# An f32 encoder layer on one core: other PSUM banks for two kinds of tile, two gain buffers, 8-block steps in the down products, and SiLU as one instruction

## The chip, the cores and the metric

The kernel runs on one core of one Trainium2 chip. The metric is device time in microseconds (us). The engines have their own instruction queues and run side by side: PE (TensorE) multiplies matrices into PSUM, DVE (VectorE) and ACT (ScalarE) work element by element, POOL (GpSimd) does a few small ones, SP (SyncE) issues the DMAs. PSUM has eight banks here, each of them one tile of 128x512 f32.

## The reference

One layer on 256 tokens of width 2048, all in f32:

```
h += 1/2 * post(SwiGLU_1(pre(h)))          # 2048 -> 5632 -> 2048
h += post(W_o [norm(NA heads) | norm(dilated heads)])   # q/k/v: 2048 -> 3*2048
h += 1/2 * post(SwiGLU_2(pre(h)))
h += post(sigmoid(pre(h) W_g) * (p W_p))   # p: 256 tokens x 256

swiglu(u)  = (silu(u @ w_gate) * (u @ w_up)) @ w_down
pre, post  = RMSNorm with a gain per column
```

The mixer has 16 heads of width 128 in four groups of four: the first group is a neighbourhood attention with a position bias, the other three a mixture of dilated windows with rotary positions. Every head's output is normalised before `W_o`.

## The kernel before, in words

Every product of weights has the 256 tokens in two halves (t = 0, 1) as the stationary operand and 512 columns of a weight as the moving one. To keep f32 precision each operand is split into a high part (a cast to the reduced type `F32R`) and a low part (the rest), and a block of 128 rows costs three matmuls: high x high (line 90), low x high (91), high x low (92). `split` does this for two row blocks of a weight: the cast `wh` on ACT (line 72), the difference `wl` on DVE (line 73). Six such pairs of buffers exist. The weights arrive by DMA as `raw` (line 64), in tiles of up to four row blocks.

`product` runs over the row blocks in steps: it loads and splits the step's blocks, then takes all of them for t = 0 and all of them for t = 1. A step has 8 blocks (`SUPER`) unless the caller gives `steps`. `mid` is a function that is called shortly before the last blocks of t = 1, when the sum of t = 0 is complete. Work put into `later` is issued behind the next step.

A feed-forward block takes the 5632 hidden columns in eleven pieces of 512, in four groups of 3, 3, 3 and 2. All but the first piece use `pair_product`, which for the first four row blocks computes gate and up together, with seven block products instead of eight, by sums and differences of operands; it has four short sums (`x = bank("x")`, each used up at once) and four long ones (v, z, y, x). `gated` then makes `silu(x) = x * sigmoid(x)`, with the row factor `rs[t]` of the norm in `scale`. Behind each group come its down products, four blocks of 512 columns each (loop over `b`), added up in `f`. In the last group, `down_out` also takes the squares of `f` on ACT and multiplies by the post-norm's gain, which one DMA per column block brings (`gain`). `residual` is a generator that goes on from there: the factor of the norm (DVE, POOL), the update of `h` (line 328), its transposes on PE (`tr`, line 239), the gain `y_g`, and the two parts `u_h` (245) and `u_l` (246) for the next stage.

In the attention stage each group of heads does q, k and v by `product`, then `attend` for each t and each pair of heads: scores `sc` (line 504), bias and maximum on DVE (`sb`, 511), exponential on ACT (`pr`, 515), transposes `pt` (521), their copy `pts` (523), and the sum over values `o` (527), for which a tile is taken from the pool `ps_acc`.

At the start, `load_x` brings the transposed x in eight pieces of two row blocks and makes the two parts of `x * gain` while the first product runs: a product on DVE (`xg`, line 297), a cast on ACT (298), a difference on DVE (299). The pieces of the first four row blocks are kept (`x_first`) for the sums that `pair_product` needs (`token_sums`).

The order of the instructions on each engine is not written by hand: a scheduler sets it from the program, the dependencies and the free buffers. So a pool with other counts of buffers changes the order. PSUM before: six banks in `ps_acc`, used in turn by all products, the pair sums and `o`; two in `ps_tr` for scores and transposes.

## Time and profile before

| | us |
|---|---|
| median of 3 runs | 1985.33 (1981.21 to 1986.32) |
| the profiled execution | 1985.5 |
| its span, first to last instruction | 1983.5 |
| PE busy | 1947.0 |
| DVE busy | 1371.2 |
| ACT busy | 992.0 |
| first matmul at | 6.11 |

Rows of instructions have the start in us, the length in us, engine, line, operation, result <- operands, shapes and count; in brackets the idle time of the engine before it and what ended it. Rows of groups have the count, then busy time in us and mean ns of one, then the idle time before them. Busy PE is drawn by modelled ends: successive matmuls overlap in the rows. PEclk is the clock that PE was granted, 1 being full.

### The profile page before, as it was taken

To read this page: it belongs to the slowest core of one execution; us is meant where nothing else is said; L and a number is where in the kernel's file an instruction comes from. 1 tells how busy PE (TensorE), PEld (TensorE's weight loads), DVE (VectorE), ACT (ScalarE), POOL (GpSimd) and SP (SyncE) were. 2 spreads that over 40 slices of the span, in tenths; PEclk is the share of its full clock that TensorE was granted. 3 is DMA by queue.
4 is the path that set the end of the run, shared out by engine and by line. 5 is a ranking of instruction groups with operands and counts; after the bars stand their busy time and mean duration, and the time that the engine had idled before them with its cause. 6 is when DMAs were issued, how large, how long until landed. Compare 5 with 4: busy or idle time off the path is not lost.

```text
span 1983.5 us, 22804 instructions
## 1 busy us (share of the span) xinstructions
PE 1947.0 (98%) x8840; PEld 1612.7 (81%) x8840; DVE 1371.2 (69%) x1526; ACT 992.0 (50%) x1206; POOL 26.5 (1%) x47
## 2 busy tenths in 40 slices
PE   8999999999999999999999999999999999999998
PEld 6888888888888878788888878888888888888786
DVE  6874787578757776566565587747875787577764
ACT  6554554355435446544535465545543554354563
POOL 0000000000000000000000000000000000000000
PEclk9999999999999999999999999999999999999999
DMA  9666556555655546454453665555565556555453
GB/s 336 212 211 201 170 191 226 177 191 170 233 170 191 191 163 214 130 198 139 138 202 127 219 211 186 210 198 171 191 229 174 191 170 233 170 190 191 170 195 119
DMA packets 190348, 376.91 MB, mean 190 GB/s; under 512 B 6432, under 2 KB 9504, under 8 KB 189984
## 3 DMA queue, kind: packets, MB, share of 16 engines
q1 hardware_dynamic: 190240, 375.46, 55.8%
q8 instruction: 69, 1.13, 0.2%
q14 instruction: 39, 0.32, 0.0%
HBM read 373.33 MB, written 2.10 MB: 189 GB/s over the span
## 4 chain that ended last, share of the span: by engine, by line
PE 95%; DMA 2%; ACT 1%; DVE 1%; issue 0%; POOL 0%; SPq 0%; DVEq 0%; POOLq 0%; ACTq 0%
PE down L90 8%; PE down L91 8%; PE down L92 8%; PE pair_x L90 5%; PE pair_x L91 5%; PE pair_x L92 5%; PE pair_z L92 3%; PE pair_y L90 3%; PE pair_z L90 3%; PE pair_z L91 3%; PE pair_y L92 3%; PE pair_y L91 3%; PE pair_v L90 3%; PE pair_v L91 3%; PE pair_v L92 3%; PE tr L239 2%
## 5 line engine op out<-in xcount | busy, mean ns | idle before, releaser
L73 DVE TENSOR_TENSOR wl<-raw,wh 128x1024 fp32r<-128x1024 f32 (+1 forms) x753 | 908.9, 1221 | 446.0 <-ACT wh L72 421.8
L72 ACT CAST wh<-raw 128x1024 fp32r<-128x1024 f32 (+1 forms) x753 | 790.0, 1052 | 762.2 <-PE down L91 207.9
L90 PE MATMUL down<-wh,hid_h 128*128 128x512 f32 x704 | 274.7, 391 | 0.1
L91 PE MATMUL down<-wh,hid_l 128*128 128x512 f32 x704 | 274.2, 389 | 0.0
L92 PE MATMUL down<-wl,hid_h 128*128 128x512 f32 x704 | 274.2, 389 | 0.0
L90 PEld LDWEIGHTS down<-wh,hid_h 128*128 128x128 f32 x704 | 132.2, 188 | 28.1 <-ACT hid_h L245 1.0
L92 PEld LDWEIGHTS down<-wl,hid_h 128*128 128x128 f32 x704 | 132.2, 188 | 27.4
L91 PEld LDWEIGHTS down<-wh,hid_l 128*128 128x128 f32 x704 | 132.2, 188 | 27.1
L90 PE MATMUL pair_x<-wh,u_h 128*128 128x512 f32 x320 | 124.6, 389 | 0.0
L91 PE MATMUL pair_x<-wh,u_l 128*128 128x512 f32 x320 | 124.6, 389 | 0.0
L92 PE MATMUL pair_x<-wl,u_h 128*128 128x512 f32 x320 | 124.6, 389 | 0.0
L90 PE MATMUL pair_y<-wh,u_h 128*128 128x512 f32 x280 | 109.0, 389 | 0.0
L92 PE MATMUL pair_y<-wl,u_h 128*128 128x512 f32 x280 | 109.0, 389 | 0.0
L91 PE MATMUL pair_y<-wh,u_l 128*128 128x512 f32 x280 | 109.0, 389 | 0.0
L161 DVE TENSOR_TENSOR raw<-raw 128x1024 f32<-128x1024 f32 x80 | 97.8, 1223 | 1.4
L92 PE MATMUL pair_z<-wl,u_h 128*128 128x512 f32 x240 | 93.5, 390 | 0.0
L90 PE MATMUL pair_z<-wh,u_h 128*128 128x512 f32 x240 | 93.4, 389 | 0.0
L91 PE MATMUL pair_z<-wh,u_l 128*128 128x512 f32 x240 | 93.4, 389 | 0.0
L91 PE MATMUL pair_v<-wh,u_l 128*128 128x512 f32 x240 | 93.4, 389 | 0.0
L92 PE MATMUL pair_v<-wl,u_h 128*128 128x512 f32 x240 | 93.4, 389 | 0.0
L90 PE MATMUL pair_v<-wh,u_h 128*128 128x512 f32 x240 | 93.4, 389 | 0.0
L92 PEld LDWEIGHTS pair_x<-wl,u_h 128*128 128x128 f32 x320 | 60.1, 188 | 12.5
(195 smaller groups left out, 3085.3 us busy)
## 6 DMA issues: line engine op xcount, KB each, us to landing
raw<-in_ffn_w_up SPq DMA_DIRECT2D x88, 1024.0 KB, 5.1
raw<-in_ffn_w_down SPq DMA_DIRECT2D x88, 1024.0 KB, 4.9
raw<-in_ffn_w_gate SPq DMA_DIRECT2D x84, 1024.0 KB, 5.1
raw<-in_w_qkv SPq DMA_DIRECT2D x48, 1024.0 KB, 5.1
raw<-in_w_o SPq DMA_DIRECT2D x16, 1024.0 KB, 4.9
raw<-in_w_ple_gate SPq DMA_DIRECT2D x16, 1024.0 KB, 5.0
raw<-in_ffn_w_gate SPq DMA_DIRECT2D x7, 512.0 KB, 4.8
xb<-in_xT SPq DMA_DIRECT2D x8, 256.0 KB, 4.2
```

Source lines behind the costliest of these rows:

```text
L72: nc.scalar.copy(wh[:, :n], raw)
L73: nc.vector.tensor_tensor(wl[:, :n], raw, wh[:, :n].bitcast(F32), op=ALU.subtract)
L90: nc.tensor.matmul(acc, xh, wh, start=lead, stop=False)
L91: nc.tensor.matmul(acc, xl, wh, start=False, stop=False)
L92: nc.tensor.matmul(acc, xh, wl, start=False, stop=tail)
L161: nc.vector.tensor_tensor(out_, x, y, op=ALU.add)
L239: nc.tensor.transpose(tr[:, k], x[:, k * P : (k + 1) * P], ident)
```

## The change

- PSUM: `ps_acc` has 4 banks, and a new pool `ps_o` has 2, for the short sums of `pair_product` and for the attention output `o`.
- `gpool`, the gains of the post-norms, has 2 buffers, not 1.
- The down products of the second to fourth column block take the default steps (for 12 row blocks 4 and 8, for 8 row blocks 8) instead of steps of 4.
- `gated` is one ScalarE instruction (`Silu`) instead of a sigmoid on ACT and a product on DVE.
- `load_x` makes the high part on ACT straight from x with the gain as a scale, one row block at a time, and the low part by one DVE instruction each. x of the first four row blocks is multiplied by the gain in place afterwards, for the token sums.
- Some scratch tiles have another buffer name (`y0` instead of `sq`).

```diff
-    gpool = ctx.enter_context(tc.tile_pool(name="gpool", bufs=1))
+    gpool = ctx.enter_context(tc.tile_pool(name="gpool", bufs=2))
-    ps_acc = ctx.enter_context(tc.tile_pool(name="ps_acc", bufs=6, space=PSUM))
+    ps_acc = ctx.enter_context(tc.tile_pool(name="ps_acc", bufs=4, space=PSUM))
     ps_tr = ctx.enter_context(tc.tile_pool(name="ps_tr", bufs=2, space=PSUM))
+    ps_o = ctx.enter_context(tc.tile_pool(name="ps_o", bufs=2, space=PSUM))
...
         def bank(x):
+            if x == "s":
+                return ps_o.tile([P, NB], F32, name="pair_s", tag="o")
             return ps_acc.tile([P, NB], F32, name=f"pair_{x}", tag="acc")
...
-        x = bank("x")
+        x = bank("s")
         mac(x, a11, split(ra[:, :2]), first=True, last=True)
...
-        xb = work.tile([P, 2, S], F32, name="xb", tag="hg")
+        xb = work.tile([P, 2, S], F32, name="xb", tag="y0" if k < KB else "hg")
         nc.sync.dma_start(xb, xT[:, k : k + 2])
-        xg = work.tile([P, 2, S], F32, name="xg", tag="y0" if k < KB else "sq")
-        g = row_g[:, 0, k : k + 2]
-        nc.vector.tensor_tensor(xg, xb, g.unsqueeze(2).broadcast_to([P, 2, S]), op=ALU.mult)
-        nc.scalar.copy(hi, xg)
-        nc.vector.tensor_tensor(lo, xg, hi.bitcast(F32), op=ALU.subtract)
+        for i in range(2):
+            g = row_g[:, 0, k + i : k + i + 1]
+            nc.scalar.activation(hi[:, i], xb[:, i], AF.Copy, scale=g)
+            nc.vector.scalar_tensor_tensor(
+                lo[:, i], xb[:, i], g, hi[:, i].bitcast(F32), op0=ALU.mult, op1=ALU.subtract
+            )
         if k < KB:
-            x_first.append(xg)
+            x_first.append(xb)
...
         def gated(x, t):
-            s = pool.tile([P, NB], F32, name="sig", bufs=1)
-            nc.scalar.activation(s, x, AF.Sigmoid, scale=rs[t])
             y = pool.tile([P, NB], F32, name="gs", bufs=3)
-            nc.vector.scalar_tensor_tensor(y, x, rs[t], s, op0=ALU.mult, op1=ALU.mult)
+            nc.scalar.activation(y, x, AF.Silu, scale=rs[t])
             return y
...
                         product(gate, lhs, w_gate, 0, c0, steps=steps, ahead=load_x)
+                        for i, x in enumerate(x_first):
+                            g = row_g[:, 0, 2 * i : 2 * i + 2].unsqueeze(2).broadcast_to([P, 2, S])
+                            nc.vector.tensor_tensor(x, x, g, op=ALU.mult)
...
-                product(acc, hrows, w_down, f0 * NB, b * NB, steps=[KB] * ng, mid=mid)
+                product(acc, hrows, w_down, f0 * NB, b * NB, steps=[KB] * ng if b == 0 else None, mid=mid)
...
-                o = ps_acc.tile([P, KB, HD], F32, name="o", tag="acc")
+                o = ps_o.tile([P, KB, HD], F32, name="o", tag="o")
...
-                later.append(lambda on=on, t=t: transposed_split(on, *o_split, t, g))
+                later.append(lambda on=on, t=t: transposed_split(on, *o_split, t, g, tag="y0"))
```

The change moves instructions. Three places show it; line numbers of the changed program are up to 5 higher, and the number behind a PSUM tile's name tells tiles apart.

PE in the attention stage of the second head group, behind the first scores, before:

```order
L504 MATMUL sc<-kT_l,qT_h 128x256
L521 MATMUL pt<-ident,pr 128x128 x2
L504 MATMUL sc<-kT_h,qT_h 128x256
L504 MATMUL sc<-kT_h,qT_l 128x256
L504 MATMUL sc<-kT_l,qT_h 128x256
L521 MATMUL pt<-ident,pr 128x128 x2
L504 MATMUL sc<-kT_h,qT_h 128x256
L504 MATMUL sc<-kT_h,qT_l 128x256
L504 MATMUL sc<-kT_l,qT_h 128x256
L527 MATMUL o<-v,pts 128x128 x4
```

And now, from the last of the six q matmuls behind the scores on:

```order
L93 MATMUL q_6743<-wl,u_h 128x512
L526 MATMUL pt<-ident,pr 128x128 x2
L509 MATMUL sc<-kT_h,qT_h 128x256
L509 MATMUL sc<-kT_h,qT_l 128x256
L526 MATMUL pt<-ident,pr 128x128 x2
L509 MATMUL sc<-kT_l,qT_h 128x256
L509 MATMUL sc<-kT_h,qT_h 128x256
L509 MATMUL sc<-kT_h,qT_l 128x256
L509 MATMUL sc<-kT_l,qT_h 128x256
L91 MATMUL q_6743<-wh,u_h 128x512
L532 MATMUL o<-v,pts 128x128 x4
L92 MATMUL q_6743<-wh,u_l 128x512
```

The matmuls of the next group's q product, which stood behind the fourth pair of heads, now stand between: two row blocks (six matmuls, of which the last is shown) ahead of the first pt, twelve matmuls in the first head group, and one ahead of and one behind each o.

PE at the end of the first feed-forward block, before:

```order
L90 MATMUL down_5329<-wh,hid_h 128x512
L91 MATMUL down_5329<-wh,hid_l 128x512
L92 MATMUL down_5329<-wl,hid_h 128x512
L239 MATMUL tr<-ident,h 128x128 x8
L90 MATMUL q_5526<-wh,u_h 128x512
```

And now:

```order
L92 MATMUL down_5290<-wh,hid_l 128x512
L242 MATMUL tr<-ident,h 128x128 x4
L93 MATMUL down_5290<-wl,hid_h 128x512
L242 MATMUL tr<-ident,h 128x128 x4
L91 MATMUL down_5290<-wh,hid_h 128x512
L92 MATMUL down_5290<-wh,hid_l 128x512
L93 MATMUL down_5290<-wl,hid_h 128x512
L91 MATMUL q_5487<-wh,u_h 128x512
```

The two transposes of h for t = 0 now stand before the last four of the 24 down matmuls for t = 1.

ACT at the start, with what each instruction waits for, before:

```order
L298 ACT_TABLE_LOAD
L298 CAST u_h<-xg 128x512 [waits DVE_49]
L72 CAST wh<-raw 128x512 [waits DMAHW2_49]
L72 CAST wh<-raw 128x512 [waits DMAHW3_49]
L298 CAST u_h<-xg 128x512 [waits DVE_49]
```

And now; DMAHW1 is the first piece of x, DMAHW0 the row gains:

```order
L300 ACT_TABLE_LOAD [waits DMAHW1_49]
L300 ACTIVATE u_h<-xb,row_g 128x256 [waits DMAHW0_49]
L300 ACTIVATE u_h<-xb,row_g 128x256
L73 CAST wh<-raw 128x512 [waits DMAHW2_49]
L73 CAST wh<-raw 128x512 [waits DMAHW3_49]
L300 ACTIVATE u_h<-xb,row_g 128x256 [waits DMAHW4_49]
```

The table load waits for x now. On DVE, the token sums stand ahead of the split of row blocks 4 and 5 (the last row); before, they stood behind the last piece of x:

```order
L373 TENSOR_TENSOR xb<-xb,row_g 128x512
L258 TENSOR_TENSOR y_s<-xb 128x256
L260 TENSOR_TENSOR y_s<-xb 128x256
L259 TENSOR_TENSOR y_s<-y_s,xb 128x256
L261 TENSOR_TENSOR y_s<-xb,y_s 128x256
L264 TENSOR_TENSOR sums_l<-y_s,sums_h 128x512
L74 TENSOR_TENSOR wl<-raw,wh 128x1024
```

## The prediction

> **What bounds the kernel now.** I read the page first, then the busy time by stretches, then what TensorE (PE) waited for, then three stretches instruction by instruction.

> From the page, PE's share and the chain that ended last:

> ```profile
> PE 1947.0 (98%) x8840; PEld 1612.7 (81%) x8840; DVE 1371.2 (69%) x1526; ACT 992.0 (50%) x1206; POOL 26.5 (1%) x47
> PE 95%; DMA 2%; ACT 1%; DVE 1%; issue 0%; POOL 0%; SPq 0%; DVEq 0%; POOLq 0%; ACTq 0%
> ```

> PE sets the end. The number of its matrix instructions does not change, so time can come only from where PE pauses or runs at less than its full clock. Two starts, 21 matmuls apart, give the slot of one 128x512 matmul when nothing holds it:

> ```profile
> 1861.66 0.39 PE L92 MATMUL down<-wl,hid_h 128*128 128x512 f32 x1
> 1866.42 0.39 PE L92 MATMUL down<-wl,hid_h 128*128 128x512 f32 x1
> ```

> (1866.42 - 1861.66) / 21 = 0.227 us. Busy time by stretches (length, then PE busy; after the five engines PEclk, the granted clock) shows where slots are lost:

> ```profile
> 50.00:400.00 350.00, 350.00 (x1570) 290.44 (x1569) 251.18 (x251) 174.03 (x186) 0.00 (x0) 1.00 0.58 197
> 0.00:40.00 40.00, 32.07 (x125) 24.90 (x126) 26.85 (x36) 23.65 (x33) 1.48 (x9) 1.00 0.92 320
> 720.00:740.00 20.00, 16.36 (x69) 12.48 (x68) 15.62 (x23) 7.53 (x12) 2.81 (x4) 0.83 0.37 130
> 800.00:820.00 20.00, 16.70 (x98) 14.43 (x97) 9.57 (x26) 13.28 (x27) 1.02 (x1) 0.91 0.34 106
> 880.00:900.00 20.00, 17.83 (x111) 15.25 (x110) 9.57 (x26) 12.57 (x27) 1.01 (x1) 1.00 0.42 140
> 1860.00:1880.00 20.00, 16.62 (x72) 13.35 (x71) 13.12 (x19) 10.46 (x17) 3.29 (x4) 0.91 0.53 184
> ```

> Inside a feed-forward block PE has no gap in 350 us. The loss sits at the start, at the end of the first feed-forward block (720), in the attention stage of the first head group (800) and of the three that follow like the one at 880, and at the end of the second feed-forward block (1860). Loss = gap + (1 - PEclk) x 20: 3.6 + 3.4 = 7.0 us at 720, 3.3 + 1.8 = 5.1 at 800, 2.2 at 880, 3.4 + 1.8 = 5.2 at 1860.

> **The change part by part.**

> *Own PSUM banks for the attention output and the short pair products.* What PE waited for in attention, over all four stages (total us, times, longest), and the rows of the stage at 880:

> ```profile
> PE pt L521 <- ACT pr L515: 6.5, 4, 2.7
> PE o L527 <- ACT pts L523: 3.5, 11, 0.7
> 806.12 1.28 ACT L515 ACT_TABLE_LOAD   x1
> 886.37 1.23 DVE L73 TENSOR_TENSOR wl<-raw,wh 128x1024 fp32r<-128x1024 f32 x1
> 887.26 0.28 PE L504 MATMUL sc<-kT_l,qT_h 128*128 128x256 f32 x1
> 888.82 0.44 PE L521 MATMUL pt<-ident,pr 128*128 128x128 f32 x2 [1.28 <-ACT pr L515]
> 889.46 0.38 PE L521 MATMUL pt<-ident,pr 128*128 128x128 f32 x2
> 890.51 0.49 PE L527 MATMUL o<-v,pts 128*128 128x128 f32 x2 [0.32 <-ACT pts L523]
> 896.75 0.48 PE L90 MATMUL q<-wh,u_h 128*128 128x512 f32 x1
> 897.07 0.39 PE L91 MATMUL q<-wh,u_l 128*128 128x512 f32 x1
> ```

> After the scores (sc) PE stands until softmax (pr) is there; the longest of the four, 2.7, holds the table load of 1.28. The new order puts matmuls of the next product (q, in the last group mo) into these places: six behind the first scores (twelve in the first group), then one before and one behind each o. Six need 6 x 0.227 = 1.36 us against a wait of 1.28; twelve 2.72 against 2.7. The o waits for pts, 1.05 us after the second pt (889.46 to 890.51). In the new order two pt, four sc and one q stand between, about 0.2 + 0.5 + 0.3 = 1.0 (lengths of the starts above). So nearly all 6.5 + 3.5 = 10.0 us of waiting go. A row of 0.28 is followed after 0.11 to 0.12 when nothing holds PE, so each of the 15 waits hides about 0.16 more: 2.4. The half-rate time at 800 (1.8) should go with its wait. Against this, the first 128x512 matmul behind a narrow one takes 0.32 (896.75 to 897.07), not 0.227: 0.09 for some 6 more switches in each of 4 stages, 2.2. Sum 10.0 + 2.4 + 1.8 - 2.2 = 12.0. The weights must be split by then: the wl at 886.37 ended before the scores did, and DVE's and ACT's order in this stage is unchanged. Bounds: 6 if half of the fills come late, 12; I take **-11**.

> *Longer steps in the down products (8 row blocks, 4 for the first column block).* The token half t=0 now ends 24 matmuls before the product does, not 12. At the end of the first block:

> ```profile
> 724.03 0.69 DVE L396 TENSOR_TENSOR f<-f,down 128x512 f32<-128x512 f32 x1 [0.63 <-PE down L92]
> 725.56 0.69 DVE L399 TENSOR_TENSOR f<-f,g_post 128x512 f32<-128x512 f32 x1 [0.85 <-ACT sq L232]
> 726.32 0.39 PE L92 MATMUL down<-wl,hid_h 128*128 128x512 f32 x1
> 728.17 1.41 DVE L328 SCALAR_TENSOR_TENSOR h<-f,r,h 128x512 f32<-128x512 f32 x2 [0.44 <-POOL r L227]
> 729.02 1.71 PE L239 MATMUL tr<-ident,h 128*128 128x128 f32 x8 [2.31 <-issue]
> 731.56 0.80 PE L90 MATMUL q<-wh,u_h 128*128 128x512 f32 x1 [0.82 <-ACT u_h L245]
> 732.04 1.29 DVE L246 TENSOR_TENSOR u_l<-y_g,u_h 128x512 fp32r<-128x512 f32 x2
> ```

> From the add of f at 724.03 (call it F) to the first transpose is 4.99 us. PE began its t=1 half 0.2 before F and was out of work 2.5 after it. Now the first transpose stands behind 20 matmuls, 4.5 us: the wait falls from 2.5 to about 0.7. What is late next: from the transpose to the first q is 2.54 us, and eight transposes and four matmuls (0.9 + 0.9) cover 1.8 of it, leaving 0.7. Then u_l: in the new DVE order the add of f for t=1, which needs the product's end (F + 7.2), and an h update stand ahead of it, so u_l ends near F + 9.3 and the second q waits about 1.6. Only one split for q stands ahead of all this; the next one follows u_l and costs about 1.0. Waits of 0.7 + 0.7 + 1.6 + 1.0 = 4.0 against 7.0 lost now: 3.0 if no half-rate time follows, 1.3 if one does (the two stretches at 0.91 lost 1.8 each). I take **-2.5**, bounds 0 and -5.

> [...]

> *Two buffers for the post-norm gains.* At the end of the second block:

> ```profile
> 1859.31 0.34 SPq L217 DMA_DIRECT2D g_post<-in_ffn_post_g  x1
> 1864.12 0.69 DVE L396 TENSOR_TENSOR f<-f,down 128x512 f32<-128x512 f32 x1 [0.63 <-PE down L92]
> 1868.49 0.69 DVE L399 TENSOR_TENSOR f<-f,g_post 128x512 f32<-128x512 f32 x1 [3.68 <-DMA g_post<-in_ffn_post_g]
> 1871.99 0.63 PE L239 MATMUL tr<-ident,h 128*128 128x128 f32 x4 [3.38 <-DVE h L328]
> ```

> The gain arrived 2.8 us later in the chain than in the first block (4.37 after F instead of 1.53). With two buffers it is asked for one column block earlier, some 11 us. Then the chain is the first block's 4.99, and the wait before the transposes 0.7 instead of 3.4; behind them stand 48 matmuls of the small projection, 10.9 us, which cover u_h and u_l. Half rate (1.8) goes. 3.4 + 1.8 - 0.7 = 4.5, less some switches of 0.09: **-4**, bounds -2 and -5.

> *Start: the scaled copy on ACT.* The rows of today:

> ```profile
> 0.71 1.28 ACT L298 ACT_TABLE_LOAD   x1 [0.71 <-PEq L722]
> 3.90 0.69 DVE L297 TENSOR_TENSOR xg<-xb,row_g 128x512 f32<-128x512 f32 x1 [3.90 <-DMA xb<-in_xT]
> 5.44 1.26 ACT L72 CAST wh<-raw 128x512 fp32r<-128x512 f32 x2 [0.19 <-DMA raw<-in_ffn_w_gate]
> 6.11 0.80 PE L90 MATMUL gate<-wh,u_h 128*128 128x512 f32 x1 [6.11 <-ACT wh L72]
> 8.12 0.80 PE L91 MATMUL gate<-wh,u_l 128*128 128x512 f32 x1 [1.22 <-DVE u_l L299]
> L515 ACT ACTIVATE pr<-sb,nmax 128x256 f32<-128x256 f32 x32 | 16.0, 499 | 4.6 <-DVE nmax L511 3.4 <-DVE sso L537 1.1
> L255 DVE TENSOR_TENSOR y_s<-xg 128x256 f32<-128x256 f32 x1 | 0.4, 422 | 0.0
> L354 DVE SCALAR_TENSOR_TENSOR gs<-p,r,sig 128x512 f32<-128x512 f32 x20 | 15.0, 752 | 15.8 <-ACT sig L352 15.8
> ```

> The table load is the first ACT instruction, and in the new order it waits for the first piece of x. So: x at 3.9, load to 5.1, two scaled copies of 128x256 at 0.45 (the exponential of that size takes 0.50, and 0.62 is half of the two casts of 128x512 above) to 6.0, wh to 6.7: the first matmul comes 0.6 later. The 1.2 at 8.12 goes, because u_l no longer stands behind the next x; at half rate that frees two or three slots. But both engines' orders now have the token sums (six DVE and two ACT instructions, 4 us of DVE by 0.69 and 0.4 each) before the splits of row blocks 4 and 5, which puts PE back by 1. Together **+0.5**, bounds -1 and +2.

> *One ScalarE instruction for the gate.* It removes 44 DVE instructions (gs, the last row above) of 0.75, 33 us of DVE, and leaves 44 on ACT. PE has no wait for the gate (the 350 us without a gap hold it), so 0. If that cover were gone, the gate would be worth at most 0.75 for each of 22 blocks. ACT's order shows five table loads, not four: the sigmoid of the last stage needs its own. 1.28 on an engine busy for half of the span: 0. [...] The trace shows 1.28, and the copy that follows a load at once.

> Sum: -11 - 2.5 - 4 + 0.5 = -17, against the profiled execution's 1985.5 (span 1983.5 and 2.0 around it). The median of the runs shown is 1985.33, so the two stand together: **1968 us**.

> **The rivals.**

> *Half of the fill only* (chance 0.20). The softmax chain, not the order, sets the attention stage: a matmul put between can hold pt or o longer than the wait it fills. For it: margins of 0 to 0.1 us in the sums above. Against it: ACT and DVE are idle for a third to a half of that stretch. Attention then gives 5: 1974.

> *The ends give nothing* (0.12). The waits move from the transposes to u_h and u_l, half rate stays, and the start costs its 2. Then -11 + 2: 1976.5.

> *Longer steps starve PE* (0.04). A step of 8 holds four of the six split pairs for its whole second half; if the casts for the next step come late, each of 24 such steps (3 in each of 8 groups) waits. At 0.7 us a step the gain is gone, at 1.0 us it is +24: 1992. Against it, the same step of 8 runs today in the output projection without a gap:

> ```profile
> L90 PE MATMUL mo<-wh,hid_h 128*128 128x512 f32 x128 | 50.2, 392 | 0.0
> ```

> The casts need 4 x 1.2 us of DVE in each 10.9 us.

> *It is not one instruction* (0.02): the gate function would swap tables with the casts at each block, 88 x 1.28 us of ACT. Five loads in the order speak against it; time then over 1990.

> **How the numbers follow.** My forecast has 0.62 and its own range is 1963 to 1974. With the first two rivals the range for 8 in 10 is 1962 to 1978. A change under about 0.3% (6 us) can't be told from none here; faster than 1979.4 has 0.88 (forecast, both rivals, less their upper edges), within 0.3% 0.07, slower 0.05.

> **What would show it.** Right: in attention no wait of pt for pr over 0.3 us and the granted clock 1.00 in all four stages; before the first transposes of each block's end a wait under 1 us; no wait of DVE for a gain; the first matmul near 6.7. Wrong: waits of down matmuls for wh or wl; pt still waiting over 1 us; PE waiting over 1.5 us for u_l with the clock below 1.

## The result and the profile after

The changed kernel takes 1967.16 us (median of 4 runs, 1966.55 to 1969.06), the kernel before beside it 1984.55 (4 runs, 1981.21 to 1986.32): a ratio of 0.9916, with a 95% interval of 0.9899 to 0.9933. The profiled execution took 1969.06, its span is 1967.0, against 1985.5 and 1983.5 before. So 16.5 us of span are gone. Two executions in this document, 2800.57 us with the earlier start and 7008.73 us (the profiled one) with the old gate, were in a slow state and are left out of the times and ratios.

The page of the changed kernel, busy time by engine and the chain that ended last:

```profile
PE 1941.9 (99%) x8840; PEld 1607.5 (82%) x8840; DVE 1340.8 (68%) x1484; ACT 994.5 (51%) x1215; POOL 28.3 (1%) x47
...
PE 96%; DVE 2%; DMA 1%; ACT 0%; issue 0%; POOL 0%; SPq 0%; DVEq 0%; POOLq 0%; ACTq 0%
```

PE still sets the end. DVE has 30 us less to do. What PE waited for (total us, times, longest):

```profile
PE gate L91 <- ACT wh L73: 8.8, 2, 7.0
PE q L91 <- ACT u_h L248: 1.5, 1, 1.5
PE tr L242 <- DVE h L332: 1.0, 2, 0.5
PE q L93 <- DVE wl L74: 1.0, 1, 1.0
```

The waits of pt for pr and of o for pts, 10.0 us before, are no longer there. Busy time by stretches, at the places that the prediction spoke of (by the add of f, the end of the first block comes 1.2 us earlier now and that of the second 15.4):

```profile
0.00:40.00 40.00, 31.16 (x118) 24.57 (x119) 25.01 (x38) 24.28 (x41) 0.97 (x9) 0.96 0.90 320
720.00:740.00 20.00, 17.26 (x85) 13.25 (x84) 15.47 (x25) 7.70 (x12) 3.28 (x4) 1.00 0.46 157
800.00:820.00 20.00, 20.00 (x121) 16.92 (x120) 10.15 (x27) 13.89 (x28) 1.01 (x1) 1.00 0.32 106
880.00:900.00 20.00, 20.00 (x121) 16.98 (x121) 11.22 (x31) 12.50 (x27) 2.01 (x2) 1.00 0.32 106
...
1840.00:1870.00 30.00, 28.99 (x138) 23.69 (x137) 25.08 (x34) 19.70 (x30) 2.81 (x4) 1.00 0.55 184
```

The attention stages at 800 and 880 have no gap. The granted clock is 1.00 from 21.74 to 1960.51, behind the last matmul.

Where the time went, place by place. Loss here is a sum over the matmuls of a stretch: the time from each start to the next, less what the same width takes where nothing holds PE (0.227 us for 512 columns, 0.109 for 128, 0.119 for 256: the medians of the trace). Half rate, a granted clock of 0.50, is in it.

| loss, us | before | after | change | predicted |
|---|---|---|---|---|
| start: first matmul's time, and loss to 40 us | 11.8 | 13.3 | +1.5 | +0.5 |
| end of the first block | 7.35 | 5.50 | -1.9 | -2.5 |
| four attention stages | 16.34 | 4.55 | -11.8 | -11 |
| end of the mixer | 2.71 | 2.62 | -0.1 | not spoken of |
| end of the second block | 5.20 | 1.54 | -3.7 | -4 |

Together -16.0. The 96 score matmuls, whose median went from 0.125 to 0.119, are -0.6 more; the rest is +0.1.

The second head group's attention, after the first scores:

```profile
883.29 0.39 PE L93 MATMUL q<-wl,u_h 128*128 128x512 f32 x1
...
883.42 0.50 ACT L520 ACTIVATE pr<-sb,nmax 128x256 f32<-128x256 f32 x1
883.57 0.44 PE L526 MATMUL pt<-ident,pr 128*128 128x128 f32 x2
...
884.54 0.58 ACT L528 COPY pts<-pt 128x512 f32<-128x512 f32 x1 [0.53 <-PE pt L526]
...
884.82 0.39 PE L91 MATMUL q<-wh,u_h 128*128 128x512 f32 x1
...
885.18 1.16 PE L532 MATMUL o<-v,pts 128*128 128x128 f32 x8
```

The second head's exponential starts at 883.42, when the first's is done; pt for the first follows 0.15 later, straight behind the sixth q, and o starts 0.06 behind the end of the copy (884.54 + 0.58 = 885.12). The fill only just covers, as worked out. The end of the first block:

```profile
722.80 0.69 DVE L401 TENSOR_TENSOR f<-f,down 128x512 f32<-128x512 f32 x1 [2.34 <-PE down L93]
...
726.95 2.08 DVE L332 SCALAR_TENSOR_TENSOR h<-f,r,h 128x512 f32<-128x512 f32 x3 [0.44 <-POOL r L230]
727.80 0.63 PE L242 MATMUL tr<-ident,h 128*128 128x128 f32 x4 [0.51 <-issue]
...
728.95 1.28 DVE L246 TENSOR_TENSOR y_g<-tr,row_g 128x512 f32<-128x512 f32 x2
...
729.70 1.04 ACT L73 CAST wh<-raw 128x1024 fp32r<-128x1024 f32 x1 [1.95 <-PE down L92]
...
730.65 1.14 ACT L248 CAST u_h<-y_g 128x512 fp32r<-128x512 f32 x2
...
731.32 0.50 PE L91 MATMUL q<-wh,u_h 128*128 128x512 f32 x1 [1.48 <-ACT u_h L248]
...
746.69 1.23 DVE L446 TENSOR_TENSOR na_bias<-na_bias,na_mask 128x1024 f32<-128x1024 f32 x1 [1.61 <-DMA na_bias<-in_na_bias]
...
750.17 2.36 DVE L74 TENSOR_TENSOR wl<-raw,wh 128x1024 fp32r<-128x1024 f32 x2
```

From the add of f to the first transpose it is 5.00 us (predicted 4.99), but from there to the first q 3.52 instead of the 2.54 that the prediction took over from before: DVE updates h for a third column block before it turns to y_g, and on ACT a cast of a weight stands ahead of u_h. The last two rows are a wait that the prediction had not named: the weights' split stands in DVE's queue behind an addition to the attention bias, and that waits for its DMA; PE then stands for 1.16 us. The end of the second block:

```profile
1848.75 0.69 DVE L401 TENSOR_TENSOR f<-f,down 128x512 f32<-128x512 f32 x1 [2.33 <-PE down L93]
1850.29 0.69 DVE L404 TENSOR_TENSOR f<-f,g_post 128x512 f32<-128x512 f32 x1 [0.85 <-ACT sq L235]
...
1853.79 0.63 PE L242 MATMUL tr<-ident,h 128*128 128x128 f32 x4 [0.54 <-DVE h L332]
```

The multiplication by the gain waits for the squares and no longer for a DMA; it comes 1.54 behind the add of f instead of 4.37, and the chain takes 5.04 us instead of 7.87. The start:

```profile
4.22 1.28 ACT L300 ACT_TABLE_LOAD   x1 [4.22 <-DMA xb<-in_xT]
...
6.99 0.79 PE L91 MATMUL gate<-wh,u_h 128*128 128x512 f32 x1 [6.99 <-ACT wh L73]
...
15.04 0.62 ACT L263 CAST sums_h<-y_s 128x512 fp32r<-128x512 f32 x1 [3.00 <-DVE y_s L259]
...
16.66 0.50 PE L91 MATMUL gate<-wh,u_h 128*128 128x512 f32 x1 [1.79 <-ACT wh L73]
```

The table load stands behind x, and the token sums hold ACT for 3.0 us ahead of a weight's cast for which PE then waits 1.8.

### The profile page after: what moved, and what is told of

Same layout as the page of the kernel before. It is cut to its first block, busy times and chain, and to the rows that moved or that the text cites. A ratio compares the mean times of both kernels' runs of the same rounds, so it can differ in the third digit from the quotient of the medians.

```text
span 1967.0 us, 22833 instructions
## 1 busy us (share of the span) xinstructions
PE 1941.9 (99%) x8840; PEld 1607.5 (82%) x8840; DVE 1340.8 (68%) x1484; ACT 994.5 (51%) x1215; POOL 28.3 (1%) x47
## 4 chain that ended last, share of the span: by engine, by line
PE 96%; DVE 2%; DMA 1%; ACT 0%; issue 0%; POOL 0%; SPq 0%; DVEq 0%; POOLq 0%; ACTq 0%
PE down L91 8%; PE down L93 8%; PE down L92 8%; PE pair_z L93 3%; PE pair_x L91 3%; PE pair_y L91 3%; PE pair_z L92 3%; PE pair_x L92 3%; PE pair_y L92 3%; PE pair_z L91 3%; PE pair_x L93 3%; PE pair_y L93 3%; PE pair_v L92 3%; PE pair_v L91 3%; PE pair_v L93 3%; PE pair_s L92 2%
## 5 line engine op out<-in xcount | busy, mean ns | idle before, releaser
L73 ACT CAST wh<-raw 128x1024 fp32r<-128x1024 f32 (+1 forms) x753 | 790.1, 1052 | 728.5 <-PE pair_z L92 178.5
L91 PE MATMUL down<-wh,hid_h 128*128 128x512 f32 x704 | 274.7, 391 | 0.2
L92 PE MATMUL down<-wh,hid_l 128*128 128x512 f32 x704 | 273.9, 389 | 0.0
L91 PEld LDWEIGHTS down<-wh,hid_h 128*128 128x128 f32 x704 | 132.2, 188 | 28.1 <-ACT hid_h L248 1.1
L92 PEld LDWEIGHTS down<-wh,hid_l 128*128 128x128 f32 x704 | 132.2, 188 | 27.1
L91 PE MATMUL pair_y<-wh,u_h 128*128 128x512 f32 x280 | 108.9, 389 | 0.0
L92 PE MATMUL pair_y<-wh,u_l 128*128 128x512 f32 x280 | 108.9, 389 | 0.0
L91 PE MATMUL pair_x<-wh,u_h 128*128 128x512 f32 x280 | 108.9, 389 | 0.0
L92 PE MATMUL pair_x<-wh,u_l 128*128 128x512 f32 x280 | 108.9, 389 | 0.0
L93 PE MATMUL pair_x<-wl,u_h 128*128 128x512 f32 x280 | 108.9, 389 | 0.0
L91 PE MATMUL pair_v<-wh,u_h 128*128 128x512 f32 x240 | 93.4, 389 | 0.0
L92 PE MATMUL pair_v<-wh,u_l 128*128 128x512 f32 x240 | 93.4, 389 | 0.0
L91 PE MATMUL pair_z<-wh,u_h 128*128 128x512 f32 x240 | 93.4, 389 | 0.0
L92 PE MATMUL pair_z<-wh,u_l 128*128 128x512 f32 x240 | 93.4, 389 | 0.0
L401 DVE TENSOR_TENSOR f<-f,down 128x512 f32<-128x512 f32 x48 | 32.8, 683 | 44.4 <-PE down L93 44.4
```

Of the source, the lines that this page charges most:

```text
L73: nc.scalar.copy(wh[:, :n], raw)
L91: nc.tensor.matmul(acc, xh, wh, start=lead, stop=False)
L92: nc.tensor.matmul(acc, xl, wh, start=False, stop=False)
L93: nc.tensor.matmul(acc, xh, wl, start=False, stop=tail)
L401: nc.vector.tensor_tensor(f_t, f_t, acc[t], op=ALU.add)
```

## The experiments

All are the changed kernel with one thing altered. Losses in us are from each one's profile, as above, at the start, the end of the first block, the four attention stages and the end of the second block; the ratio is against the kernel before, run beside it.

| | times, us | ratio (95%) | start | first end | attention | second end |
|---|---|---|---|---|---|---|
| the change | 1966.6 to 1969.1 | 0.9916 (0.9899 to 0.9933) | 13.3 | 5.5 | 4.6 | 1.5 |
| shared banks | 1976.9 to 1981.3 | 0.9969 (0.9956 to 0.9982) | 11.4 | 4.3 | 15.4 | 1.5 |
| short sums in shared banks | 1967.3 to 1968.8 | 0.9907 (0.9893 to 0.9922) | 13.3 | 5.2 | 4.5 | 1.6 |
| pts copied twice | 1966.9 to 1969.8 | 0.9909 (0.9894 to 0.9925) | 12.4 | 6.1 | 4.0 | 1.5 |
| steps of four | 1969.5 to 1971.2 | 0.9920 (0.9906 to 0.9935) | 11.2 | 8.3 | 4.4 | 1.5 |
| one gain buffer | 1966.6 to 1968.9 | 0.9907 (0.9891 to 0.9924) | 12.7 | 4.6 | 4.5 | 1.7 |
| steps of four, one gain buffer | 1972.5 to 1975.3 | 0.9940 (0.9922 to 0.9958) | 13.1 | 8.1 | 4.3 | 5.1 |
| gain multiplied later | 1967.1 to 1969.9 | 0.9910 (0.9895 to 0.9926) | 13.6 | 5.7 | 4.5 | 1.8 |
| small projection split | 1971.0 to 1971.6 | 0.9925 (0.9908 to 0.9942) | 12.4 | 8.0 | 4.5 | 1.7 |
| old start | 1966.9 to 1968.7 | 0.9907 (0.9892 to 0.9922) | 12.3 | 5.9 | 4.7 | 1.6 |
| earlier start | 1965.3 to 1967.3 | 0.9901 (0.9884 to 0.9919) | 10.0 | 5.9 | 4.5 | 1.5 |
| earlier start, projection split | 1968.2 to 1971.5 | 0.9916 (0.9902 to 0.9931) | 10.9 | 10.1 | 4.5 | 1.7 |
| old gate | 1966.1 to 1966.6 | 0.9899 (0.9883 to 0.9916) | | | | |

### The banks

```diff
-    ps_acc = ctx.enter_context(tc.tile_pool(name="ps_acc", bufs=4, space=PSUM))
+    ps_acc = ctx.enter_context(tc.tile_pool(name="ps_acc", bufs=6, space=PSUM))
-    ps_o = ctx.enter_context(tc.tile_pool(name="ps_o", bufs=2, space=PSUM))
...
-                return ps_o.tile([P, NB], F32, name="pair_s", tag="o")
+                return ps_acc.tile([P, NB], F32, name="pair_s", tag="acc")
...
-                o = ps_o.tile([P, KB, HD], F32, name="o", tag="o")
+                o = ps_acc.tile([P, KB, HD], F32, name="o", tag="acc")
```

> The changed kernel with the banks undone alone: six banks for everything, o and the short pair sums among them. Loss is the time between the starts of successive matmuls above that of matmuls which nothing holds (0.227 us for 128x512). Theory (the order decides: with o in the shared banks the matmuls of the next product stand behind the fourth pair of heads, and PE waits for softmax): the loss in the four attention stages goes from 4.6 back to 16.3 us, pt waits for pr four times (6.5 in all), half rate follows in the first stage, and the time is about 11.8 us above 1967, near 1979. Rival (the softmax chain sets the stage, half of the fills came late): 5 us, near 1972.

What PE waited for in this kernel:

```profile
PE pt L525 <- ACT pr L519: 6.5, 4, 2.7
PE o L531 <- ACT pts L527: 3.6, 12, 0.4
```

Both waits are back, within 0.1 us of those before, the attention loss is 15.4, and the time rises by 10 to 14 us. The order of PE's instructions in these stages is that of the kernel before. The theory holds, the rival's 5 us don't. One part came out otherwise: the first stage had the same wait of 2.7 and no half rate (a granted clock of 1.00 from 795 to 815, against 0.91 in the kernel before); the last section comes back to that.

In the second run only `o` has banks of its own:

```diff
             if x == "s":
-                return ps_o.tile([P, NB], F32, name="pair_s", tag="o")
+                return ps_acc.tile([P, NB], F32, name="pair_s", tag="acc")
```

> The changed kernel with the short pair sums back in the pool of the products (four banks), and o alone in its own two banks. Theory (only o's banks matter: the order of PE is the same instruction by instruction): loss in the attention stages 4 to 5 us, time within 1 us of 1967. Rival (the short sums need their own banks: with four shared banks a new sum waits until an older one is added up): PE waits for pair sums in each of 20 blocks, 0.3 us each or more, 6 us or more.

Nothing is lost (attention 4.5, no wait of the pair products), and PE's order is that of the changed kernel in the whole program. So own banks for `o` are enough for the gain; those of the short sums bring nothing. The first run went back from four banks for the products to six as well; four banks shared by all were not run, so that it is the separation, and not the smaller count, is argued from the order and not shown.

The third run lengthens the softmax chain:

```diff
                     nc.scalar.copy(pts, pt)
+                    nc.scalar.copy(pts, pt)
```

> The changed kernel, with the copy pts made twice in attention: 32 more ACT instructions of 0.58 us in the chain from pt to o, where o now starts 0.06 us behind the end of the copy. Work is added that nothing needs. Theory (with its own banks the next product fills whatever the order foresees: three more of its matmuls stand ahead of each o): loss in the attention stages rises by less than 2 us over 4.6. Rival (the softmax chain sets these stages and the fill only just covers it): each of the 32 copies delays an o by about 0.5, some 16 us, near 1983.

There are 16 such copies, not 32 as the expectation says (one for each pair of heads), so the rival's price is 16 x 0.5 = 8 us. The loss in attention is 4.0, less than without the extra work. Rows of this kernel:

```profile
885.52 0.59 ACT L528 COPY pts<-pt 128x512 f32<-128x512 f32 x1 [0.53 <-PE pt L526]
...
886.14 0.59 ACT L529 COPY pts<-pt 128x512 f32<-128x512 f32 x1
...
886.49 0.39 PE L91 MATMUL q<-wh,u_h 128*128 128x512 f32 x1
...
886.78 1.16 PE L533 MATMUL o<-v,pts 128*128 128x128 f32 x8
```

Four q matmuls stand ahead of this o now, not one, and o starts 0.05 behind the second copy. So the margin of 0.06 in the changed kernel does not look like luck: here too the scheduler put in about as much of the next product as the longer wait needed.

### The ends of the feed-forward blocks

Longer steps and the second gain buffer, undone singly and together:

```diff
-                product(acc, hrows, w_down, f0 * NB, b * NB, steps=[KB] * ng if b == 0 else None, mid=mid)
+                product(acc, hrows, w_down, f0 * NB, b * NB, steps=[KB] * ng, mid=mid)
```

> The changed kernel with steps of four row blocks in all down products, as before. Theory: at the end of the first block the transposes wait about 2.5 us again, the loss there goes from 5.5 to about 7.3, half rate included; at the end of the second block, with two gain buffers, the transposes wait up to 2.5 us. Together 2 to 4 us above 1967. Rival (the steps move only the wait from the transposes to the next u_h and u_l): within 1 us of 1967.

The first end is back at 8.3 (of it, by the list of waits, the 2.3 ahead of the transposes, and half rate: a granted clock of 0.83 from 720 to 740), the second stays at 1.5, and the time rises by about 3 us. The theory holds for the first end; at the second, undoing the steps alone costs nothing.

The single gain buffer:

```diff
-    gpool = ctx.enter_context(tc.tile_pool(name="gpool", bufs=2))
+    gpool = ctx.enter_context(tc.tile_pool(name="gpool", bufs=1))
```

> The changed kernel with one buffer for the post-norm gains instead of two. Theory (the gain is asked for when the multiplication of the column block before is done, and that is set by the end of that block's product, so the longer steps cannot cover it): at the end of the second block the transposes wait about 3 us again, the loss there goes from 1.5 back to about 5, the time is 3.5 us above 1967; the first block's end, where the gain came in time before, may lose as well. Rival (the 12 more matmuls that now stand ahead of the transposes cover the late gain): 0 to 1 us.

This theory fell. The loss at the second end is 1.7, and the time does not change. The rows there:

```profile
1844.90 0.34 SPq L220 DMA_DIRECT2D g_post<-in_ffn_post_g  x1
...
1847.20 0.69 DVE L401 TENSOR_TENSOR f<-f,down 128x512 f32<-128x512 f32 x1 [2.33 <-PE down L93]
...
1849.85 1.42 DVE L332 SCALAR_TENSOR_TENSOR h<-f,r,h 128x512 f32<-128x512 f32 x2 [0.95 <-POOL r L230]
...
1850.74 1.29 PE L242 MATMUL tr<-ident,h 128*128 128x128 f32 x8 [0.18 <-DVE h L332]
1851.18 0.69 DVE L404 TENSOR_TENSOR f<-f,g_post 128x512 f32<-128x512 f32 x1
```

The gain is late, as the theory said: its DMA lands 6.2 us after the issue, at 1851.1, 3.9 behind the add of f. But the multiplication by it (last row) now stands behind the first updates of h, which need only the first two column blocks, and so nothing waits for it. From the add of f to the first transpose it is 3.54 us (3.50 at the first end, where the order is changed in the same way and the loss is 4.6). The new theory, that either edit alone is enough at the second end, had its own run:

> The changed kernel with one gain buffer and steps of four, so both edits undone that were meant to help the ends of the feed-forward blocks; undone one by one, either left the loss at the end of the second block at 1.5 to 1.7 us. Theory (either edit alone is enough there, each in its own way: two buffers bring the gain in time; with one buffer and longer steps the multiplication by the gain stands behind the first updates of h on DVE, so that nothing waits for it): with both gone the multiplication stands ahead of the updates again and waits for the gain, the loss there is 5 us, at the first block's end 7 to 8, and the time is 3.5 us above that with the steps alone undone (1970.6), near 1974. Rival (the second block's end was helped by something else in the change, the banks or the start): loss there stays near 1.5, time near 1970.6.

With both undone PE waits again, as this kernel's list says:

```profile
PE tr L242 <- DVE h L332: 3.5, 2, 3.0
PE tr L242 <- issue: 2.3, 1, 2.3
```

The second end loses 5.1, the first 8.1, and the median is 1974.56 against the 1974 expected. So these two edits together are worth 7.4 us (1974.56 - 1967.16). The steps alone are worth 3.5 of it (1970.62 - 1967.16), at the first end; the other 3.9 are the second end, which either edit earns (3.6 by the profile, 5.1 - 1.5).

If the multiplication is what lengthens the chain, it can be put behind in the program as well:

```diff
                         squares(f_t, ssf[t][:, b : b + 1])
-                        nc.vector.tensor_tensor(f_t, f_t, gp, op=ALU.mult)
+                        if t == 1 or b < D // NB - 1:
+                            nc.vector.tensor_tensor(f_t, f_t, gp, op=ALU.mult)
...
                         next(res)
+                        f_t = f[:, 0, b * NB : (b + 1) * NB]
+                        nc.vector.tensor_tensor(f_t, f_t, gp, op=ALU.mult)
```

> The changed kernel, and in the last column block the multiplication of t=0 by the gain is put behind the first updates of h and their transposes in the program, since these need only the first two column blocks. Theory (that multiplication, 0.69 us on DVE, is on the chain from the sum to the transposes, and so are the split and the POOL operations that run beside it): the chain from the add of f to the first transpose shortens from 5.0 to about 3.5 us, the transposes wait 0.3 or less at both blocks' ends, the first q waits less, the loss at the first end goes from 5.5 to about 4.5, time 1 to 1.5 us below 1967. Rival (PE's wait only moves to u_h and u_l): 0.

The rival holds: the first end loses 5.7. The chain to the first transpose is 3.88 us instead of 5.00 (the multiplication now runs while POOL works), but the order draws the transposes forward by as much, so that they wait 0.68 as before; the first q loses 0.28 instead of 1.65, and the second the more (1.14 instead of 0.60). The wait has moved to u_l.

Is that remainder there because PE has nothing else to do? At the second end it has the small projection. Half of that (`EARLY` is 2 column blocks) was moved to the first end, ahead of what is left of `residual` (`p1` is p with its two parts):

```diff
+    keep = ctx.enter_context(tc.tile_pool(name="keep", bufs=1, space=bass.MemoryType.DRAM))
+    kept = keep.tile([P, EARLY * NT, NB], F32, name="kept")
...
+        for b in range(EARLY):
+            acc = accs("pp")
+            product(acc, [(p1[1][:, k], p1[2][:, k]) for k in range(PLE // P)], a["w_ple_proj"], 0, b * NB, jobs=False)
+            for t in range(NT):
+                y = pool.tile([P, NB], F32, name="pp", tag="part", bufs=6)
+                nc.scalar.copy(y, acc[t])
+                nc.sync.dma_start(kept[:, b * NT + t], y)
...
-    for b in range(D // NB):
+    for i in range(EARLY * NT):
+        y = pool.tile([P, NB], F32, name="pp", bufs=NT * D // NB)
+        nc.sync.dma_start(y, kept[:, i])
+        pp.append(y)
+    for b in range(EARLY, D // NB):
```

> The changed kernel, and half of the small projection (p W_p, column blocks 0 and 1, 24 matmuls or 5.4 us of PE) is done at the end of the first feed-forward block instead of the second; its result is kept in DRAM and read back at the end. Theory (what is left at the first block's end, 5.5 us against 1.5 at the second's, is there because PE has no other work while u_h and u_l are made; the second has 48 matmuls of this projection): the waits of the first and second q (1.65 and 0.6) and the transposes of t=1 go, the loss there falls from 5.5 to about 2.5, the second block's end stays at about 1.5 with the 24 that are left, together 3 us below 1967. Rival (the split of the q weights on DVE, late at 750, and the longer queue on DVE and ACT set it): 0 to 1.

The cover works: the waits of the first and second q are gone, and the loss from 720 to 740 falls from 3.9 to 1.6. But the kernel is slower, for the wait that had cost 1.16 at 750 costs 4.6, and half rate follows it for 3.41 us, which costs 1.7:

```profile
745.14 0.93 SPq L458 DMA_DIRECT2D na_bias<-in_na_bias  x2
...
750.26 1.23 DVE L460 TENSOR_TENSOR na_bias<-na_bias,na_mask 128x1024 f32<-128x1024 f32 x1 [3.72 <-DMA na_bias<-in_na_bias]
...
754.23 0.79 PE L94 MATMUL q<-wl,u_h 128*128 128x512 f32 x1 [4.47 <-DVE wl L75]
```

The attention bias is asked for at 745.1, 5 us later than in the changed kernel, and DVE stands for it with the weights' split behind. It is late because SP, which issues it, stands for 7.9 us just ahead of it, at the first of the loads of biases (L450), until the projection's result has been written to DRAM:

```profile
SPq L450 <- DMA kept<-pp: 7.9, 1, 7.9
```

So neither story was whole: PE's lack of work makes the first part of the remainder, and DVE's queue behind a late DMA the second; the growth of this second part from 1.16 to 4.6 goes with the writes that this experiment itself adds. The same kernel without these writes, or with the addition behind the splits, was not run.

### The start

The old start in the changed kernel undoes the diff of `load_x` shown above.

> The changed kernel with the start as before: gain product on DVE, cast on ACT, token sums behind the last piece of x. Theory: first matmul at 6.1 instead of 7.0, no wait of 1.95 at 14.5, no second stretch of half rate; the loss of the first 40 us goes from 6.3 to 5.7, together 1.5 us below 1967. Rival (the start is bound by the arrival of x and the weights, so that later waits give it back): 0.

The first matmul is at 5.9 (theory 6.1), but u_l then holds the second for 2.4 us, and the sum is 12.3 against 13.3; the time does not move. Profiles with the new start's code, unchanged by their edit, are nine, and their starts cost 11.2 to 13.6, 12.6 on average; the two with the old one cost 11.8 and 12.3. A difference of 0.6 between averages lies well inside the 2.4 by which one and the same code varies, so the 1.5 of the profiled execution cannot be called shown. Part of what varies is half rate: six of the nine profiles have a stretch of it behind the wait at 14.5, like the changed kernel's (a granted clock of 0.96 over the first 40 us), and their starts cost 12.4 to 13.6; the three without it (1.00) cost 11.2 to 12.4, and neither profile of the old start has one (1.00).

Both causes that the rows name can be taken away:

```diff
     nc.gpsimd.memset(mhalf, -0.5)
+    warm = const.tile([P, 1], F32, name="warm")
+    nc.scalar.copy(warm, mhalf[:, :1])
...
+                        with tc.issue_after(last_u[0].ins), tc.issue_after(last_u[1].ins):
                             for i, x in enumerate(x_first):
...
```

`last_u` holds the last instruction of u_h on ACT and of u_l on DVE; the products of `x_first` and the token sums are put behind them.

> The changed kernel with two edits at the start: a small copy on ACT that depends on nothing from outside, so that the table load does not wait for x, and the token sums placed behind the last piece of x on ACT and DVE. Theory (the start lost 1.5 us to the table load behind x and to the token sums ahead of the split of row blocks 4 and 5): first matmul at 6.1 instead of 7.0, no wait of 1.95 at 14.5 and no second stretch of half rate, the loss of the first 40 us from 6.3 to about 3.5, together 3 to 3.5 us below 1967. Rival (the arrival of x and weights sets it): first matmul 0 to 0.5 earlier, the wait at 14.5 stays, 0 to 0.5 us.

The first matmul is at 6.03, the wait at 14.5 and the second stretch of half rate are gone, and the start costs 10.0, less than in any of the eleven profiles just counted. So the two causes together are real; which of them brings how much was not taken apart. In time it is about 1 us, too little to tell from none with these intervals.

### Both edits together

> The same with the two edits of the start (table load not behind x, token sums behind the last piece of x), which took 3 us from the loss of the first 40 us in the profile and 1 us from the median. Theory (the two lie at different places and add up): 4 us below 1967, near 1963; loss in the first 40 us about 4 with the first matmul at 6.0, at the first block's end about 2.5. Rival (they do not add up): 1965 to 1967.

They don't add up; the wait for the weights' split is 5.9 here (SP waits 8.0 for the writes), and the first end loses 10.1. The start keeps its gain (10.9). No version here is faster than the changed kernel by more than can be measured.

### The gate

```diff
+            s = pool.tile([P, NB], F32, name="sig", bufs=1)
+            nc.scalar.activation(s, x, AF.Sigmoid, scale=rs[t])
             y = pool.tile([P, NB], F32, name="gs", bufs=3)
-            nc.scalar.activation(y, x, AF.Silu, scale=rs[t])
+            nc.vector.scalar_tensor_tensor(y, x, rs[t], s, op0=ALU.mult, op1=ALU.mult)
```

> The changed kernel with the gate function as before, a sigmoid on ACT and a product on DVE. Theory (the gate lies beside PE's matmuls; 44 DVE instructions of 0.75 come back, 33 us of DVE, and one table load of 1.28 goes): no row of PE waits for gs or hm, time within 1 us of 1967. Rival (DVE is close to the limit in the pair products, 9 tenths in the busiest slices): PE waits for wl in the blocks, up to 0.75 for each of 22 blocks, 16 us.

1966.1 to 1966.6: the old gate costs nothing. Its profile is that of the execution left out, so the waits that the expectation speaks of were not seen, only the times.

## Why the prediction was right, and where not

- **Own banks for `o`, -11.** -11.8 in the profile, +10.9 when undone. The mechanism held: no wait of pt or o is left, and the switches between narrow and wide matmuls are in the 4.6 that remain (the first wide one behind a narrow one takes 0.32 us here too, 886.09 to 886.41). The half-rate time of 1.8 that it counted for the first stage is not always there: the kernel with shared banks had the wait without it. The rival, half of the fill only, is refuted twice, by the undone banks and by the lengthened chain. Its strongest point, margins of 0 to 0.1 us, was read the wrong way round: with the chain made longer by 0.6, the margin was again 0.05.
- **Longer steps, -2.5.** -1.9, and 2.7 when undone (8.25 - 5.50). The wait ahead of the transposes is 0.67 (0.7 predicted). Behind it the sum of 4.0 was wrong in its parts. The first q waited 1.65 and not 0.7: the stretch from the transpose to the first q, 2.54 taken over from before, measured 3.52, because the new order puts an update of h and a cast ahead of y_g and u_h. Against that the second q waited 0.60 and not 1.6, and the next split, put at 1.0, held nothing. Two waits were not named: 0.59 of the transposes for t = 1, and the 1.16 at 750, which is a later split behind the attention bias and its DMA. With 0.8 of small pieces they make the 5.5. That no half rate followed is luck: three other profiles had it behind the same waits (a granted clock of 0.91 from 720 to 740; see the last section).
- **Two gain buffers, -4.** The size was right (-3.7), and the wait before the transposes is 0.70 as forecast; the cause was half of it. The step that failed is that the late gain needs the second buffer. With the longer steps, one buffer does as well, since the order then puts the multiplication behind what it had held up (undone alone, the buffers cost nothing: 1.7 at that end). The prediction looked at when the gain arrives and not at whether the updates of h need it.
- **The start, +0.5.** +1.5 in this execution, 0.6 between averages. Both mechanisms were right: the table load behind x, and the token sums ahead of a split. The first matmul came at 6.99 and not near 6.7, for x landed at 4.22 instead of 3.90, and the second stretch of half rate was not foreseen.
- **The gate, 0.** Confirmed.
- **The other rivals.** No down product waits for a weight, so the steps starve nothing, and ACT has five table loads in all. The ends, which the second rival held to give nothing, gave 5.5 (1.85 + 3.66).
- **The sum.** 1967.16 against 1968 is closer than the parts, and that is luck: the start lost 1.0 more than forecast and the ends gave 0.6 and 0.3 less, while attention gave 0.8 more and the score matmuls, which the sum did not hold, 0.6.

## What to carry to other kernels

Where an engine whose order is set beforehand waits for a chain on others, look for the next piece of independent work, and for the buffer that keeps it from being put there: here two PSUM banks for one tile were worth some 11 of the 16.5 us. Before a late operand is fetched earlier, ask who needs the result: here the multiplication that waited at the head of a queue was put behind the others at no cost. Two edits that each cure the same wait don't add up, and only undoing both shows what they are worth.

## What the runs showed of the hardware

```profile
726.42:729.83 3.41, 1.02 (x7) 0.55 (x6) 2.88 (x4) 1.10 (x2) 1.63 (x2) 1.00 0.43 166
729.83:733.24 3.41, 2.16 (x6) 1.25 (x7) 3.41 (x6) 1.84 (x4) 0.00 (x0) 0.50 0.01 2
...
804.93:808.34 3.41, 0.71 (x7) 0.51 (x5) 2.39 (x6) 3.38 (x7) 0.00 (x0) 1.00 0.92 286
808.34:811.75 3.41, 3.38 (x17) 3.08 (x16) 0.78 (x4) 1.64 (x6) 0.00 (x0) 0.50 1.00 322
...
1869.89:1873.30 3.41, 1.30 (x10) 1.25 (x11) 2.69 (x5) 0.00 (x0) 1.09 (x2) 1.00 0.21 79
1873.30:1876.71 3.41, 3.41 (x9) 2.65 (x9) 3.32 (x6) 2.59 (x5) 0.00 (x0) 0.50 0.00 0
```

In the step ahead of 808.34 PE was busy for 0.71 of 3.41 us (0.21), and it ran the next one at half rate. In the kernel with shared banks the same wait of 2.7 was followed by none: the granted clock is 1.00 from 795 to 815. Where steps of 3.4133 us (1064.96 / 312) would lie there is an estimate from the start of the program. In the kernel before, the matmuls go from 0.43 to 0.23 us apart at about 13.05, 233 steps ahead of 808.34 (the profile gives a clock of 1.00 on both sides of that); with shared banks they do so at about 11.96, and 11.96 + 231 x 3.4133 = 800.4:

```profile
800.43:803.85 3.42, 1.49 (x10) 1.17 (x8) 3.29 (x7) 3.10 (x4) 0.00 (x0) 1.00 0.60 161
```

Busy for 0.44 of this step and 0.68 of the next (2.32 of 3.41), PE kept its full clock, and the first stage lost 4.9 instead of 5.9. At the first block's end, the kernel with the old start had half rate and the changed kernel had not, with the same waits of 0.67, 1.65 and 0.60; steps of the old start (two) and of the changed kernel:

```profile
729.03:732.44 3.41, 1.81 (x7) 1.28 (x8) 3.41 (x8) 2.37 (x5) 0.01 (x1) 1.00 0.00 0
732.44:735.86 3.42, 3.42 (x10) 2.68 (x9) 2.70 (x4) 0.00 (x0) 1.64 (x2) 0.50 0.54 135
...
728.30:731.71 3.41, 1.94 (x11) 1.11 (x9) 3.41 (x7) 2.01 (x4) 0.00 (x0) 1.00 0.00 0
```

The earlier start and the copy made twice had it there as well (a granted clock of 0.91 from 720 to 740, like the old start, against 1.00), and these three ends lost 5.9, 5.9 and 6.1 against 5.5. Half rate followed steps in which PE was busy for 0.21, 0.30 and 0.38 (the kernel before, from 804.93, 726.42 and 1869.89), 0.47 (the changed kernel, 1.60 of the 3.42 from 14.91) and 0.53 (the old start); it did not follow 0.44 and 0.68 (shared banks) and 0.57 (the changed kernel). So these steps show no sharp line in this measure, which counts matmuls by their modelled ends. Whether half rate that comes and goes is also why the kernel with shared banks spreads over 4.4 us and the changed one over 2.5 is not shown: only one execution of each has a profile.

**A POOL operation took 1.45 us beside a DVE split and 0.55 without one.** At the end of the first block of the changed kernel the power on one column took 1.45 us while a split ran on DVE, and 0.55 a little later:

```profile
725.28 1.23 DVE L74 TENSOR_TENSOR wl<-raw,wh 128x1024 fp32r<-128x1024 f32 x1 [0.18 <-ACT wh L73]
...
725.46 1.45 POOL L230 TENSOR_TENSOR r<-m,mhalf 128x1 f32<-128x1 f32 x1
...
734.62 0.55 POOL L230 TENSOR_TENSOR r<-m,mhalf 128x1 f32<-128x1 f32 x1
```

The split ends at 726.51, and the power 0.40 later. Of the 16 such powers in this trace, the two that began while a split ran (725.46 and 1851.41) took 1.45 and the other 14 took 0.55 to 0.56. It lies on the chain to the transposes. With the multiplication and the split behind it (one gain buffer) the same operation took 0.55 at the second end (at 1849.26), and that chain 3.54 us instead of 5.04.
